# All weights of the first modulation asked for first, one of its eight row pieces summed on TensorE, and the first casts of h on ScalarE

## The chip, the cores and the metric

The kernel runs on one core of one Trainium2 chip. The core has five engines that run side by side, each through its own list of instructions in a fixed order: TensorE (PE in the profile, its weight loads PEld), VectorE (DVE), ScalarE (ACT), GpSimd (POOL) and SyncE (SP), which here only asks for transfers (DMAs). The metric is the device time of one execution in microseconds (us); less is better.

## The reference

One layer of a decoder trunk over 2048 positions of width 1024. The part that the change touches is the beginning: the modulation of the input c, the normed and modulated input h, and the first projection.

```python
c_act = jax.nn.silu(c)
mod = c_act @ w_ada[l] + b_ada[l]
sh1, sc1, gt1, sh2, sc2, gt2 = [m[:, None, :] for m in jnp.split(mod, 6, axis=-1)]
h = rms_norm(x, g_mix[l]) * (1.0 + sc1) + sh1
y = hybrid_mixer(h, w_in[l], ...)      # p = h @ w_in, then attention, mLSTM, spatial gating, w_out
x = x + gt1 * y
h = rms_norm(x, g_ffn[l]) * (1.0 + sc2) + sh2
x = x + gt2 * conv_ffn(h, w_up[l], w_conv[l], b_conv[l], w_down[l])
```

The matrix w_ada is 1024 x 6144. Only the columns of sh1 and sc1 (the first 2048) are needed before h exists.

## The kernel before

**Precision.** A product of two float32 matrices is made of three: each operand is split into a high part in a reduced format (a cast: hh, wh) and the rest (a subtraction: hl, wl), and `mm3` (lines 53 to 56) issues high x high, high x low and low x high into one PSUM bank.

**The first modulation.** `first_mod(hf)` makes half of sh1 and sc1: hf = 0 gives the columns for row pieces 0 to 3 of h, hf = 1 those for pieces 4 to 7. For each of its two column groups n (512 columns of w_ada) `load_ada` asks for eight tiles wa of 128 rows x 512 columns, 256 KB each, one for each row piece k of c. `mod_sum` on DVE adds them up, each row weighted by cs, the column of silu(c) (one instruction a tile, lines 418 and 420), into modacc; four products with a column of ones (line 441) then add over the 128 rows and leave the result as columns in PSUM. Three small DVE instructions (lines 445 to 447) make sh1 and a1, the scale. The 24 short rows of b_ada and g_mix are turned on PE (line 393) and copied (line 396) for this.

**h.** `make_h(tb)` works on a block of 512 positions. `norm_x` norms four x tiles of 128 positions: two squares with sums on ACT (jk, line 518), small DVE steps, a power on POOL (line 128), and the scaling on DVE (line 523). For each of eight row pieces k PE turns four 128 x 128 tiles (line 560), ACT applies a1 and sh1 (h, line 564), DVE casts (hh, line 565) and subtracts (hl, line 566). Block 0 takes pieces k = 0 to 3 from the first half of the modulation and k = 4 to 7 from the second.

**The first projection.** The weights of the first column block (256 columns of km and 16 gate columns: 272) come as wr, two requests for each of eight row pieces (line 585); ACT casts them (wh, line 595), POOL subtracts (wl, line 596). Then 24 products of 272 columns per 128 positions make one tile acc, which ACT copies out (ev, line 661), while DVE takes the gates. Eight such tiles use blocks 0 and 1; the next column block has products of 512 columns.

**Beside it** stand small set-up steps: casts of the identity, of selector rows and of two masks (identb, selb, maskb, maskT; maskf takes the buffer that the 24 rows had), and `head_setup`, which turns the spatial weights wsn on PE (line 549) and copies them on ACT (wT, line 550).

**What sets the order.** Up to the second column block a planner orders the instructions of each engine from the code and its own costs; from there on, the order is as written. All DMAs go through SP's list, so a request that must wait holds those behind it. Tiles come from pools with a fixed number of buffers: wa, hh and hl share 32 (hT); modacc, h and later weights share four (t2k).

## Time and profile before

| what | value |
|---|---|
| median of 3 runs | 2607.26 us (2603.63 to 2610.91) |
| profiled execution | 2607.8 us, of which the span from first to last instruction is 2606.1 us |
| TensorE busy | 2530.5 us, 97% of the span |
| VectorE busy | 2010.0 us, 77% |
| ScalarE busy | 1272.8 us, 49% |
| GpSimd busy | 402.5 us, 15% |
| chain that ended last | PE 81%, DVE 9%, DMA 4%, ACT 3% |

The page gives shares over the whole span; the change lies in the first 80 us, so the views to read are the stages of the opening, the instructions in order of time there (columns: start, time, engine, line, operation, out<-in, shape, count, and in brackets the idle time of the engine before it with what ended it), and the groups of equal instructions (busy time, mean, idle before). Where a row holds several instructions (x8), its time is that from the first start to the last end. A row's time includes what of it overlaps the next; the pace of products is read from the distance of their starts.

### The profile page before, as it was taken

To read this page: it belongs to the slowest core of one execution; us is meant where nothing else is said; L and a number is where in the kernel's file an instruction comes from. 1 tells how busy PE (TensorE), PEld (TensorE's weight loads), DVE (VectorE), ACT (ScalarE), POOL (GpSimd) and SP (SyncE) were. 2 spreads that over 40 slices of the span, in tenths; PEclk is the share of its full clock that TensorE was granted. 3 is DMA by queue.
4 is the path that set the end of the run, shared out by engine and by line. 5 is a ranking of instruction groups with operands and counts; after the bars stand their busy time and mean duration, and the time that the engine had idled before them with its cause. 6 is when DMAs were issued, how large, how long until landed. Compare 5 with 4: busy or idle time off the path is not lost.

```text
span 2606.1 us, 36311 instructions
## 1 busy us (share of the span) xinstructions
PE 2530.5 (97%) x12521; PEld 2097.9 (81%) x12537; DVE 2010.0 (77%) x3438; ACT 1272.8 (49%) x2424; POOL 402.5 (15%) x532
## 2 busy tenths in 40 slices
PE   5999999999999999999989999999999999999999
PEld 5888888888787877777868888888888888888787
DVE  7657666476388889866589888888888887997797
ACT  4333343432388878844455544454444444444443
POOL 2012310132266556520000000000000000000000
PEclk9999999999999999999999999999999999999999
DMA  7345763454664445266632222255222217658523
GB/s 247 107 120 160 209 209 88 129 152 138 180 164 123 129 126 166 58 195 224 248 89 92 79 89 82 81 201 187 90 81 81 90 65 279 210 176 290 184 93 117
DMA packets 302592, 379.58 MB, mean 146 GB/s; under 512 B 31934, under 2 KB 194588, under 8 KB 300360
## 3 DMA queue, kind: packets, MB, share of 16 engines
q1 hardware_dynamic: 302408, 377.26, 46.1%
q8 instruction: 99, 1.62, 0.3%
q14 instruction: 85, 0.70, 0.1%
HBM read 276.44 MB, written 100.74 MB: 145 GB/s over the span
## 4 chain that ended last, share of the span: by engine, by line
PE 81%; DVE 9%; DMA 4%; ACT 3%; issue 2%; POOL 1%; SPq 0%; DVEq 0%; ACTq 0%; POOLq 0%
PE ub L56 11%; PE ub L54 11%; PE ub L55 11%; PE acc L54 6%; PE acc L56 6%; PE acc L55 6%; PE db L55 4%; PE db L56 4%; PE db L54 4%; PE sp L206 3%; PE tp L259 3%; PE op L245 2%; PE op L246 2%; PE wps L55 2%; PE wps L54 2%
## 5 line engine op out<-in xcount | busy, mean ns | idle before, releaser
L54 PE MATMUL acc<-wh,hh 128*128 128x512 f32 (+2 forms) x768 | 285.5, 373 | 1.9 <-DVE vhl L762 1.2
L54 PE MATMUL ub<-T,wsph 128*128 128x512 f32 x704 | 274.2, 390 | 5.8 <-ACT wsph L1358 5.8
L56 PE MATMUL ub<-T,wspl 128*128 128x512 f32 x704 | 273.7, 389 | 1.6 <-DVE wspl L1359 1.6
L56 PE MATMUL acc<-wh,hl 128*128 128x512 f32 (+2 forms) x768 | 274.2, 360 | 0.3 <-DVE hl L566 0.3
L55 PE MATMUL acc<-wl,hh 128*128 128x512 f32 (+2 forms) x768 | 273.9, 358 | 0.2
L55 PE MATMUL ub<-T,wsph 128*128 128x512 f32 x704 | 273.9, 389 | 0.0
L55 PE MATMUL db<-wspl,wsph 128*128 128x512 f32 x616 | 240.6, 391 | 3.6 <-DVE wspl L1490 3.5
L56 PE MATMUL db<-wsph,wspl 128*128 128x512 f32 x616 | 239.6, 389 | 0.0
L54 PE MATMUL db<-wsph 128*128 128x512 f32 x616 | 238.3, 389 | 0.3 <-ACT wsph L1489 0.3
L1358 ACT CAST wsph<-S 128x512 fp32r<-128x512 f32 x176 | 109.7, 623 | 228.4 <-PE ub L55 162.8
L263 DVE TENSOR_TENSOR plo<-tp,phi 128x512 fp32r<-128x512 f32 (+1 forms) x320 | 187.0, 607 | 31.6 <-ACT phi L262 29.4
L54 PE MATMUL ub<-B,wsph 128*128 128x512 f32 x528 | 207.1, 392 | 2.8 <-ACT wsph L1358 2.8
L56 PE MATMUL ub<-B,wspl 128*128 128x512 f32 x528 | 207.2, 392 | 0.6 <-DVE wspl L1359 0.6
L55 PE MATMUL ub<-B,wsph 128*128 128x512 f32 x528 | 207.0, 392 | 0.0
L223 ACT ACTIVATE L<-L,nm 128x1024 f32<-128x1024 f32 (+2 forms) x192 | 172.6, 903 | 36.0 <-DVE nm L212 34.7
L262 ACT CAST phi<-tp 128x512 fp32r<-128x512 f32 (+1 forms) x320 | 160.0, 521 | 40.2 <-PE tp L259 38.9
L259 PE MATMUL tp<-ident,L 128*128 128x128 f32 x1088 | 177.0, 274 | 2.5 <-POOL L L228 0.6
L206 PE MATMUL sp<-kk,q 128*128 128x512 f32 (+3 forms) x640 | 169.2, 375 | 3.3 <-DVE nm L212 2.2
L1489 ACT CAST wsph<-act 128x512 fp32r<-128x512 f32 x132 | 82.3, 623 | 179.0 <-PE db L55 162.2
L228 POOL TENSOR_SCALAR L<-L,rs 128x1024 f32<-128x1024 f32 (+2 forms) x192 | 167.2, 881 | 11.0
L56 PEld LDWEIGHTS acc<-wh,hl 128*128 128x128 f32 x768 | 145.0, 190 | 22.3 <-DVE hl L566 0.8
L54 PEld LDWEIGHTS acc<-wh,hh 128*128 128x128 f32 x768 | 146.2, 191 | 20.7 <-DVE vhl L762 1.4
(333 smaller groups left out, 5942.9 us busy)
## 6 DMA issues: line engine op xcount, KB each, us to landing
w<-in_w_up_dram SPq DMA_DIRECT2D x88, 512.0 KB
wd<-in_w_down_dram SPq DMA_DIRECT2D x176, 256.0 KB
wa<-in_w_ada_dram SPq DMA_DIRECT2D x96, 256.0 KB
act_d<-yc SPq DMA_DIRECT2D x44, 512.0 KB
act<-act_d SPq DMA_DIRECT2D x44, 512.0 KB
wr<-in_w_in_dram SPq DMA_DIRECT2D x64, 256.0 KB
q<-q_d SPq DMA_DIRECT2D x128, 128.0 KB
hc_d<-hl SPq DMA_DIRECT2D x28, 512.0 KB
```

The lines of the kernel that those rows point to most:

```text
L54: T.matmul(ps, lh, rh, start=start, stop=False, skip_group_check=resume)
L55: T.matmul(ps, lh, rl, start=False, stop=False, skip_group_check=resume)
L56: T.matmul(ps, ll, rh, start=False, stop=stop, skip_group_check=resume)
L206: T.matmul(sp[:, b : b + bw], q2[n][:, qs], kk[:, s0 + b : s0 + b + bw], start=n == 0, stop=n == 1 and not last)
L223: A.activation(L[c], L[c], AF.Exp, bias=nm[:, n - 1 : n], scale=-1.0, accum_out=rs[:, c : c + 1])
L228: G.tensor_scalar(t, t, rs[:, 0:1], 1.0, op0=ALU.mult, op1=ALU.mult)
L245: T.matmul(op[:, c0:], vv[:, j, :], hi[:, c0:], start=(j == 0), stop=False)
L259: T.transpose(tp[:, i * P : (i + 1) * P], rows[i][j // 8][:, (j % 8) * P : (j % 8 + 1) * P], ident)
L262: A.copy(hi[:, c0:], tp[:, c0:])
L263: V.tensor_tensor(lo[:, c0:], tp[:, c0:], hi[:, c0:].bitcast(F32), op=ALU.subtract)
L1358: A.copy(hi, src)
L1489: A.copy(hi, v)
```

## The change

- Both halves of the modulation ask for their 32 wa tiles before the first column weights. The 16 gate columns come in one request (gw) and are copied into the eight weight tiles by POOL; SP's list has 16 wa, 2 rows, 16 wa, gw, 8 wr where it had 16 wa, 2 rows, 16 wr, 16 wa.
- Of the eight row pieces of each column group DVE sums seven; the eighth goes to PE: four products of the wa tile itself with the column of cs. All products add onto a bank that DVE has set to zero.
- The eight hh casts of block 0 move from DVE to ACT.
- The casts of identb, selb, maskb and maskT move from DVE to POOL.

The order on DVE at the end of the second half of the modulation, before. Each modacc_409 row is one step of the sum of its second column group, with the wa tile that it takes; h32_446, h32_457 and h32_468 are row pieces 0 to 2 of h in block 0 with their hh and hl; sh1 and a1 are shift and scale:

```order
L420 SCALAR_TENSOR_TENSOR modacc_409<-wa_419,cs_92,modacc_409 128x512
L565 CAST hh_447<-h32_446 128x512
L420 SCALAR_TENSOR_TENSOR modacc_409<-wa_422,cs_92,modacc_409 128x512
L566 TENSOR_TENSOR hl_448<-h32_446,hh_447 128x512
L420 SCALAR_TENSOR_TENSOR modacc_409<-wa_425,cs_92,modacc_409 128x512
L565 CAST hh_458<-h32_457 128x512
L420 SCALAR_TENSOR_TENSOR modacc_409<-wa_428,cs_92,modacc_409 128x512
L566 TENSOR_TENSOR hl_459<-h32_457,hh_458 128x512
L420 SCALAR_TENSOR_TENSOR modacc_409<-wa_431,cs_92,modacc_409 128x512
L565 CAST hh_469<-h32_468 128x512
L445 TENSOR_TENSOR sh1_89<-mps_166,colA_86 128x4
L446 TENSOR_TENSOR a1_88<-mps_166,colA_86 128x4
```

And with the change, where the sum is modacc_437 and pieces 0 to 3 are h32_461, h32_472, h32_483 and h32_494:

```order
L446 SCALAR_TENSOR_TENSOR modacc_437<-wa_309,cs_92,modacc_437 128x512
L579 TENSOR_TENSOR hl_463<-h32_461,hh_462 128x512
L446 SCALAR_TENSOR_TENSOR modacc_437<-wa_311,cs_92,modacc_437 128x512
L579 TENSOR_TENSOR hl_474<-h32_472,hh_473 128x512
L446 SCALAR_TENSOR_TENSOR modacc_437<-wa_313,cs_92,modacc_437 128x512
L579 TENSOR_TENSOR hl_485<-h32_483,hh_484 128x512
L453 TENSOR_TENSOR sh1_89<-mps_166,colA_86 128x4
L454 TENSOR_TENSOR a1_88<-mps_166,colA_86 128x4
L579 TENSOR_TENSOR hl_496<-h32_494,hh_495 128x512
L455 SCALAR_TENSOR_TENSOR a1_88<-a1_88,colA_86 128x4
```

The casts are gone from DVE's list, only the subtractions (hl) still stand among the steps, and each group's sum is one step shorter.

The order on ACT from the second half's h (pieces 4 to 7) to the statistics jk of the next four x tiles, before:

```order
L564 ACTIVATE h_490<-trp,sh_89,a_88 128x512
L564 ACTIVATE h_501<-acc,sh_89,a_88 128x512
L564 ACTIVATE h_512<-trp,sh_89,a_88 128x512
L564 ACTIVATE h_523<-acc,sh_89,a_88 128x512
L550 COPY wT<-mp 128x512
L518 ACTIVATE jk,st<-xt 128x512 x2
L661 COPY ev<-acc 128x256
```

With the change; the row ahead of the first is h_505, piece 4:

```order
L608 CAST wh<-wr 128x272 x4
L576 CAST hh<-h_505 128x512
L608 CAST wh<-wr 128x272
L574 ACTIVATE h_516<-acc,sh_89,a_88 128x512
L574 ACTIVATE h_527<-trp,sh_89,a_88 128x512
L576 CAST hh<-h_516 128x512
L574 ACTIVATE h_538<-acc,sh_89,a_88 128x512
L576 CAST hh<-h_527 128x512
L576 CAST hh<-h_538 128x512
L674 COPY ev<-acc 128x256 x2
L560 COPY wT<-mp 128x512
L526 ACTIVATE jk,st<-xt 128x512 x2
```

Five weight casts and the four hh casts now stand between and behind the h of the upper half (before, all eight weight casts stood ahead of the first h), and the copies of two finished tiles come ahead of wT and jk.

The order on PE around the turn of wsn, which wT copies, before (acc_689 and acc_721 are the first two tiles of 128 positions):

```order
L54 MATMUL acc_721<-wh_356,hh_469 128x272
L55 MATMUL acc_721<-wl_357,hh_469 128x272
L56 MATMUL acc_721<-wh_356,hl_470 128x272
L54 MATMUL acc_721<-wh_360,hh_480 128x272
L549 MATMUL mp_551<-ident_74,wsn_545 128x128 x4
L56 MATMUL acc_689<-wh_368,hl_503 128x272
```

With the change (acc_768 is the third tile of 128 positions):

```order
L56 MATMUL acc_768<-wh_393,hl_474 128x272
L54 MATMUL acc_768<-wh_397,hh_484 128x272
L55 MATMUL acc_768<-wl_398,hh_484 128x272
L559 MATMUL mp_566<-ident_74,wsn_560 128x128 x4
L56 MATMUL acc_768<-wh_397,hl_485 128x272
```

The turn of wsn stood behind 27 products of 272 columns and now stands behind 56. From the first product of 512 columns on, the orders of all engines are the same as before.

The diff:

```diff
-    V.tensor_copy(identb, ident)
+    G.tensor_copy(identb, ident)
...
-    def mod_sum(tiles):
-
-        acc = pool.tile([P, 512], F32, name="modacc", tag="t2k")
-        for k, st in enumerate(tiles):
-            if k == 0:
-                V.tensor_scalar(acc, st, cs[:, 0:1], None, op0=ALU.mult)
-            else:
-                V.scalar_tensor_tensor(acc, st, cs[:, k : k + 1], acc, op0=ALU.mult, op1=ALU.add)
-        return acc
...
-    def first_mod(hf):
+    V.memset(modp[:, 0:16], 0.0)
+
+    def first_load(hf):
+        return {n: list(load_ada(n * 512, "hT")) for n in (hf, 2 + hf)}
+
+    def first_mod(hf, tiles):
         for n in (hf, 2 + hf):
-            acc = mod_sum(load_ada(n * 512, "hT"))
-            for j in range(4):
-                T.matmul(modp[:, n * 4 + j : n * 4 + j + 1], acc[:, j * P : (j + 1) * P], ones[:, 0:1], start=True, stop=True)
+            acc = pool.tile([P, 512], F32, name="modacc", tag="t2k")
+
+            def add(w, col):
+                for j in range(4):
+                    T.matmul(
+                        modp[:, n * 4 + j : n * 4 + j + 1], w[:, j * P : (j + 1) * P], col,
+                        start=False, stop=True, skip_group_check=True,
+                    )
+
+            for k, st in enumerate(tiles[n]):
+                if k == 0:
+                    V.tensor_scalar(acc, st, cs[:, 0:1], None, op0=ALU.mult)
+                elif k < 7:
+                    V.scalar_tensor_tensor(acc, st, cs[:, k : k + 1], acc, op0=ALU.mult, op1=ALU.add)
+                else:
+                    add(st, cs[:, k : k + 1])
+            add(acc, ones[:, 0:1])
...
-    first_mod(0)
+    ada = first_load(0)
+    first_mod(0, ada)
+    ada = first_load(1)
...
-            V.tensor_copy(hh, h32)
+            if tb == 0:
+                A.copy(hh, h32)
+            else:
+                V.tensor_copy(hh, h32)
...
-        def load(self):
+        def load(self, n=2):
...
-            for col, wd in self.parts:
+            for col, wd in self.parts[:n]:
...
-        V.tensor_copy(selb[r : r + 4], bc(ident[r : r + 4, r : r + 4], 2, P))
+        G.tensor_copy(selb[r : r + 4], bc(ident[r : r + 4, r : r + 4], 2, P))
...
-    V.tensor_copy(maskb, m32)
+    G.tensor_copy(maskb, m32)
...
-    V.tensor_copy(maskT, bc(maskf, 1, 4))
+    G.tensor_copy(maskT, bc(maskf, 1, 4))
...
+    gw = pool.tile([P, KT, 16], F32, name="gw", tag="tmpA")
+    dma(gw, w_in[:, C_G : C_G + 16].rearrange("(k p) n -> p k n", p=P))
     for k in range(KT):
-        cur.load()
+        cur.load(1)
+        G.tensor_copy(cur.raw[k][:, 256:272], gw[:, k, :])
     for k in range(KT):
         cur.cast()
-    first_mod(1)
+    first_mod(1, ada)
```

## The prediction

> **What bounds the kernel now.** I read the page first, then the opening by stages, then its instructions in order of time.

> ```profile
> span 2606.1 us, 36311 instructions
> PE   5999999999999999999989999999999999999999
> ```

> TensorE (PE) is full in every slice of 65 us but the first, so the kernel ends as early as PE's fixed stream of products is fed. The change touches only the opening; whatever it saves or loses by the moment PE is full for good is carried to the end. The stages (columns: stretch, its length, busy time and count for PE, weight loads, VectorE (DVE), ScalarE (ACT), GpSimd (POOL), granted clock, DMA share, GB/s):

> ```profile
> 10.00:20.00 10.00, 4.13 (x16) 2.78 (x15) 8.83 (x20) 1.86 (x7) 2.42 (x4) 1.00 1.03 371
> 20.00:30.00 10.00, 3.96 (x17) 3.75 (x17) 7.81 (x14) 3.34 (x8) 6.67 (x9) 1.00 0.74 197
> 30.00:40.00 10.00, 3.32 (x16) 3.32 (x17) 9.64 (x15) 2.23 (x3) 0.83 (x2) 1.00 0.85 308
> 47.00:53.00 6.00, 6.00 (x26) 5.67 (x27) 5.08 (x12) 2.79 (x5) 0.35 (x1) 1.00 0.66 258
> 60.00:72.00 12.00, 12.00 (x96) 11.66 (x95) 11.18 (x25) 7.96 (x14) 0.55 (x1) 1.00 0.53 154
> ```

> PE is fed from 47 us on. Before that DVE is the busy engine, with the row sums of the first modulation, and it is nearly full again from 60 to 72, with the second block of h. So there are two gates, and a gain at the first is kept only if the second does not close. Does DVE wait for data in the first?

> ```profile
> L420 DVE SCALAR_TENSOR_TENSOR modacc<-wa,cs,modacc 128x512 f32<-128x512 f32 x28 | 21.6, 780 | 0.5
> 16.47 8.64 SPq L585 DMA_DIRECT2D wr<-in_w_in_dram x16
> 25.16 9.75 SPq L410 DMA_DIRECT2D wa<-in_w_ada_dram  x16
> ```

> Hardly: 0.5 us of idle before 28 sums of 780 ns. So asking for the second sixteen wa tiles at 16.5 instead of 25.2 us gains nothing by itself; I cost it at 0, covered by the sums ahead of it. The price is that wr, whose 16 requests become 9, is asked for after wa; its casts are then queued behind h, which comes back below.

> **First gate: DVE's sums, then ACT.**

> ```profile
> 24.05 0.97 DVE L839 CAST maskT<-maskf 128x512 bf16<-128x512 f32 x1 [0.18 <-POOL maskf L838]
> 24.95 2.41 DVE L420 SCALAR_TENSOR_TENSOR modacc<-wa,cs,modacc 128x512 f32<-128x512 f32 x2
> 23.99 6.84 POOL L596 TENSOR_TENSOR wl<-wr,wh 128x272 fp32r<-128x272 f32 x8
> 29.58 0.56 DVE L447 SCALAR_TENSOR_TENSOR a<-a,colA 128x4 f32<-128x4 f32 x1
> 30.06 1.06 DVE L418 TENSOR_SCALAR modacc<-wa,cs 128x512 f32<-128x512 f32 x1
> 36.54 0.48 DVE L418 TENSOR_SCALAR modacc<-wa,cs 128x512 f32<-128x512 f32 x1
> L565 DVE CAST hh<-h 128x512 fp32r<-128x512 f32 x7 | 2.9, 419 | 0.0
> ```

> First half of the modulation: two sums leave DVE (2 x 0.78 = 1.56), the mask casts go to POOL (0.97 + 0.18 of waiting, and a 0.22 one), and the two last sums, 2.41 us beside POOL's wl, go back to 1.56 since wl now comes later: 3.8 us. Against that, POOL's identity and selector casts stand ahead of the rsqrt of the x tiles, and one x scaling stands behind a later statistic: 0.7 us, an estimate from the length of one scaling (0.76, below). PE's turn of the 24 column rows now comes after the last sum instead of ahead of it: 0.3 and 0.2 for its copy. The scale a is 0.3 quicker alone (0.56 against 0.25 for the second one). Net: a is ready 2.9 us earlier, at 27.2.

> Second half: two sums (1.56) and the first two hh casts (0.84) leave DVE's queue, and the first term is 1.06 only beside POOL, 0.48 alone (0.58): 3.0 us. New beside it are POOL's late mask work and eight small gw copies, since the wait of maskf's buffer for the 24 rows now lasts until 26.6. How much these hold DVE isn't shown; the nearest rows lost 0.4 to 0.6 us per instruction beside wl. I take 0.6 in all, bounds 0 and 3. Net 2.4, in sum 5.3.

> [...]

> TensorE's added products (k = 7, four per piece) are as long as those of the sum, of which four take 1.87 us (x8 records below); three of the four groups run while PE waits for DVE, the last ahead of its sum too, so 0.

> ```profile
> 27.41 1.87 PE L441 MATMUL mps<-ones,modacc 128*128 128x1 f32 x8 [4.43 <-DVE modacc L420]
> 43.16 0.75 DVE L420 SCALAR_TENSOR_TENSOR modacc<-wa,cs,modacc 128x512 f32<-128x512 f32 x1
> 46.98 0.78 ACT L564 ACTIVATE h<-trp,sh,a 128x512 f32<-128x512 f32 x1 [5.13 <-DVE a L447]
> 48.30 0.69 DVE L566 TENSOR_TENSOR hl<-h,hh 128x512 fp32r<-128x512 f32 x1
> 48.94 0.43 PE L54 MATMUL acc<-wh,hh 128*128 128x272 f32 x1
> 49.17 0.43 PE L55 MATMUL acc<-wl,hh 128*128 128x272 f32 x1
> 63.40 0.62 ACT L595 CAST wh<-wr 128x512 fp32r<-128x512 f32 x1
> 25.87 0.42 ACT L595 CAST wh<-wr 128x272 fp32r<-128x272 f32 x1 [0.28 <-DMA wr<-in_w_in_dram]
> ```

> So the last sum ends at 43.9 - 5.3 = 38.6, and h of the fifth piece starts at 46.98 - 5.3 = 41.7. Before, its hl ended at 48.99, 2.0 later. Now ACT runs, after that h (0.68 apart), four wh casts (4 x 0.42) and hh at the price of a 128x512 cast (0.6), then DVE the hl (0.69): 3.6, so 45.3. ACT's new work thus gives back 1.6 of the 5.3. Queued behind the h that waits for a are these wh casts, and behind those POOL's wl of pieces 3 to 7 (0.75 to 0.86 each), which follow at about PE's pace; bounds for that 0 and 1. With the last product of the piece PE has 15 products done at 45.6; before, the sixteenth starts at 49.17. First gate: 3.5 us earlier (bounds 0.1 and 4.1).

> **Second gate: ACT's queue.** The statistics of the next four x tiles (jk, the squares) stand on ACT behind the copy wT, and wT waits for PE's turn of wsn.

> ```profile
> 51.89 1.05 PE L549 MATMUL mp<-ident,wsn 128*128 128x128 f32 x4
> 52.98 0.59 ACT L550 COPY wT<-mp 128x512 f32<-128x512 f32 x1 [3.21 <-PE mp L549]
> 53.46 0.64 ACT L518 ACTIVATE jk<-xt 128x512 f32<-128x512 f32 x1
> 60.88 0.76 DVE L523 TENSOR_SCALAR xt<-xt,st 128x1024 f32<-128x1024 f32 x1 [0.58 <-POOL st L128]
> 71.73 0.69 DVE L566 TENSOR_TENSOR hl<-h,hh 128x512 fp32r<-128x512 f32 x1
> 72.64 0.54 PE L56 MATMUL acc<-wh,hl 128*128 128x272 f32 x3
> 78.28 0.39 PE L54 MATMUL acc<-hh,wh 128*128 128x512 f32 x1
> 51.44 0.43 PE L56 MATMUL acc<-wh,hl 128*128 128x272 f32 x1
> 51.66 0.43 PE L54 MATMUL acc<-wh,hh 128*128 128x272 f32 x1
> 58.75 0.29 PE L54 MATMUL acc<-wh,hh 128*128 128x272 f32 x1
> 58.88 0.29 PE L55 MATMUL acc<-wl,hh 128*128 128x272 f32 x1
> ```

> From the first jk (53.46) runs one serial chain: scale xt, turn, h, hh, hl on a full DVE; its last hl ends at 72.42, PE uses it at 72.64, and the first product of the next block starts at 78.28, 24.8 us after jk. PE keeps busy with the first block's products meanwhile, and has no slack to the last hl.

> In the changed order 56 products stand ahead of the wsn turn instead of 27 (the PE rows shown above). With 15 done at 45.6, 41 remain. Starts lie 0.22 to 0.23 us apart up to about 53 us and 0.13 after, with a granted clock of 1.00 in both stretches. Before, the slow stretch lasted some 5.6 us after PE began to run without gaps (47.5). I take the same: until 51.2 PE does 23 or 24 products and the small turn of 16 rows, then 17.5 x 0.125 = 2.2, and 0.5 for wsn: 53.9, against 52.94. So jk starts 1.0 us later although PE started 3.5 us earlier. With no slow stretch, 41 x 0.125 gives 51.4 (1.5 earlier); slow throughout, 41 x 0.226 and a slow turn give 56.0 (3.1 later). I keep the middle. The chain behind jk has the same instructions, so the next block starts at 79.3: **+1.0 us**. PE alone would be there at 78.28 - 3.5 + 0.9 (1.7 us more at half pace) = 75.7; the 3.6 us between turn up as waits of PE for xt and hl, about 59 to 73 us. From that block on the orders are the same.

> Sum against the profiled execution: span 2606.1 + 1.0 = 2607.1. That execution took 2607.8, 0.5 over the median of the runs, 2607.26; the median becomes 2608.3. With the first gate's bounds (3.4 worse, 0.6 better) and the slow stretch's (2.1 worse, 2.5 better) the shift lies between -2.1 and +6.5; the runs before spread by 3.6 either way.

> **Rivals.**
> - *The first gate's gain is kept.* If PE runs at full pace early, or ACT gets through its casts faster, jk starts no later than before and the gain is what PE alone allows: 2.6 us, 2604.7. For it: PE is full from 47 us and DVE's relief is real. Against: only a jk 1 to 3 us earlier than before gives it, which needs nearly the fast bound.
> - *PE falls back to its slow pace at the second gate.* The waits are on PE, near 60 us; if the pace drops there, the 42 products behind the last hl cost 0.1 more each, 4.2 us, beside the 1.0: 2612.5, slower. It decides if PE's waits for xt join into one long gap. For it: 7.4 us without work at 29 to 37 us had slow products on both sides. Against: I expect the waits singly, some 1.6 us each, the pitch of the xt scalings.
> - *DVE is held by POOL for long.* At the bound of 3 us the first gate gains 1.1, jk comes 3.4 later: 2610.7.
> - *The early requests do nothing and the late wr starves POOL:* included, as the 0 and the bound of 1 above.

> [...]

> **Chances.** The small loss 0.55, the kept gain 0.2, the slow pace 0.1, POOL's hold 0.1, something unseen 0.05. All four prices are under 0.3% (7.8 us), about what a measurement of this kernel can tell from no change: so within it 0.77. The losses can add up (1.0 + 4.2 + 2.4 = 7.6) and run spread does the rest: slower by more 0.14. Faster by more needs three times what PE allows: 0.09, for what I may not see. The range takes the cases from 2604.7 to 2612.5 and most of the spread: 2602 to 2615.

> **What would show it.** Second a near 41.6, first h of the upper half near 41.7, sixteenth product near 45.6; ACT's wT and jk near 54 to 55; PE idle for some 3 us in pieces between 59 and 73; first 512-wide product of the next block near 79. Wrong if that product comes before 76 or after 83, if PE's idle sits elsewhere, or if stages after 100 us differ.

## The result, and the profile after

The changed kernel takes 2612.79 us in the median of 8 runs (2609.62 to 2615.10); the kernel before took 2605.93 us in the median of 8 runs beside it (2603.63 to 2610.91). The ratio is 1.0024, with a 95% interval from 1.0015 to 1.0034. That lies within the 0.3% that the prediction took as the bound of no change, but outside zero: a small loss. A second job put it at 1.0013 (1.0005 to 1.0022). Over all runs the changed kernel averages 2612.0 us (19 runs) and the kernel before 2607.9 (118 runs): 4.1 us apart, plus or minus 1.0.

Two lines of the page of the changed kernel:

```profile
span 2611.3 us, 36387 instructions
PE   6999999999999999999989999999999999999999
```

Its span is 5.2 us above the 2606.1 before. The instructions of the changed opening in order of time, with DVE, ACT and PE mixed (columns as before; of the lines named in the prediction, L455 is now the second step of a, L574 h, L559 the turn of wsn, L526 the squares):

```profile
38.31 0.74 DVE L446 SCALAR_TENSOR_TENSOR modacc<-wa,cs,modacc 128x512 f32<-128x512 f32 x1
41.16 1.24 DVE L579 TENSOR_TENSOR hl<-h,hh 128x512 fp32r<-128x512 f32 x1
42.32 0.15 DVE L455 SCALAR_TENSOR_TENSOR a<-a,colA 128x4 f32<-128x4 f32 x1
42.57 0.78 ACT L574 ACTIVATE h<-trp,sh,a 128x512 f32<-128x512 f32 x1 [2.64 <-DVE a L455]
46.30 0.47 PE L54 MATMUL acc<-wh,hh 128*128 128x272 f32 x1
53.45 0.60 PE L559 MATMUL mp<-ident,wsn 128*128 128x128 f32 x4
54.57 0.64 ACT L526 ACTIVATE jk<-xt 128x512 f32<-128x512 f32 x1
61.24 0.44 PE L570 MATMUL trp<-ident,xt 128*128 128x128 f32 x2 [0.97 <-DVE xt L531]
62.91 0.44 PE L570 MATMUL trp<-ident,xt 128*128 128x128 f32 x2 [1.23 <-DVE xt L531]
64.11 1.11 PE L570 MATMUL trp<-ident,xt 128*128 128x128 f32 x4 [0.76 <-ACT h L574]
72.95 0.69 DVE L579 TENSOR_TENSOR hl<-h,hh 128x512 fp32r<-128x512 f32 x1
80.19 0.39 PE L54 MATMUL acc<-hh,wh 128*128 128x512 f32 x1
```

The first gate opens earlier: the second half's a is ready at 42.3 instead of 46.6, and the sixteenth product starts at 46.30, before at 49.17. The second gate opens later: jk at 54.57, before 53.46. PE waits for x tiles, and the next block's first product starts 1.9 us later than before (78.28). The other 3.3 us of the span came after that, and not in one place. By the starts of the same ScalarE instructions, the changed kernel is 1.9 us behind at 200 us, 3.5 at 300, 4.1 at 1000, 7.3 at 1300, 5.6 from 1400 to 2200 and 4.9 at the end. These are stretches of 3.41 us around the waits of the opening and around the first wait behind it that costs time, in the changed kernel (columns: stretch, length, busy time of PE, PEld, DVE, ACT, POOL, granted clock, DMA share, GB/s):

```profile
60.16:63.58 3.42, 0.98 (x5) 0.40 (x4) 2.45 (x7) 1.59 (x4) 0.78 (x2) 1.00 0.12 38
63.58:66.99 3.41, 2.88 (x13) 2.88 (x14) 3.38 (x7) 2.85 (x5) 0.00 (x0) 0.50 0.56 154
66.99:70.40 3.41, 3.41 (x30) 3.41 (x30) 3.34 (x8) 2.87 (x5) 0.00 (x0) 1.00 0.48 123
213.76:217.18 3.42, 0.73 (x8) 0.75 (x8) 3.24 (x7) 1.49 (x4) 1.55 (x2) 1.00 0.88 308
217.18:220.59 3.41, 3.41 (x12) 2.73 (x11) 2.80 (x8) 0.00 (x0) 1.44 (x2) 0.50 0.16 56
```

and at the second place in the kernel before:

```profile
210.10:213.51 3.41, 1.74 (x8) 1.10 (x6) 2.87 (x7) 1.85 (x5) 2.67 (x3) 1.00 0.71 222
213.51:216.93 3.42, 2.40 (x15) 2.16 (x16) 3.34 (x7) 0.43 (x1) 1.05 (x2) 1.00 0.53 196
```

In these rows the granted clock is 1.00 or 0.50 in whole stretches of 3.41 us. In the changed kernel PE had nothing to do for 2.69 of the 3.42 us from 213.76, and the next 3.41 us ran at half clock. The kernel before has the same wait (the instruction that ended it, first before, then after):

```profile
214.53 1.06 PE L1052 MATMUL mps<-ident,hq 128*128 128x128 f32 x8 [2.69 <-DVE hq L1045]
```

```profile
216.47 1.28 PE L1065 MATMUL mps<-ident,hq 128*128 128x128 f32 x8 [2.69 <-DVE hq L1058]
```

There it lay across two stretches, 1.67 us in one and 1.02 in the next, and the clock stayed at 1.00. The next transposes of the same kind show what that cost: 296.03 before, 299.52 after, so 3.5 us apart, where the ones above are 1.9 apart.

```profile
296.03 1.09 PE L1052 MATMUL mps<-ident,hq 128*128 128x128 f32 x8 [0.88 <-DVE hq L1045]
```

```profile
299.52 1.09 PE L1065 MATMUL mps<-ident,hq 128*128 128x128 f32 x8 [0.88 <-DVE hq L1058]
```

Up to 1300 us the changed kernel's profile has half-clock stretches at 63.6, 217.2, 1029.5 and 1237.8 us; that of the kernel before has one, at 1230.7. Between 1300 and 1350 us each has three more.

### The profile page after: what moved, and what is told of

The parts are those of the page before. It is cut to its first block, busy times and chain, and to the rows that moved or that the text cites. A ratio compares the mean times of both kernels' runs of the same rounds, so it can differ in the third digit from the quotient of the medians.

```text
span 2611.3 us, 36387 instructions
## 1 busy us (share of the span) xinstructions
PE 2539.3 (97%) x12569; PEld 2107.6 (81%) x12569; DVE 2001.9 (77%) x3421; ACT 1276.7 (49%) x2432; POOL 408.5 (16%) x546
## 4 chain that ended last, share of the span: by engine, by line
PE 81%; DVE 8%; DMA 4%; issue 3%; ACT 2%; POOL 1%; SPq 0%; DVEq 0%; ACTq 0%; POOLq 0%
PE ub L56 11%; PE ub L54 10%; PE ub L55 10%; PE acc L54 6%; PE acc L55 6%; PE acc L56 6%; PE db L55 4%; PE sp L206 4%; PE db L56 4%; PE db L54 4%; PE tp L259 3%; PE op L245 2%; PE op L246 2%; PE wps L55 2%; PE wps L54 2%
## 5 line engine op out<-in xcount | busy, mean ns | idle before, releaser
L54 PE MATMUL acc<-wh,hh 128*128 128x512 f32 (+2 forms) x768 | 286.3, 375 | 1.7 <-DVE vhl L775 1.2
L54 PE MATMUL ub<-T,wsph 128*128 128x512 f32 x704 | 274.3, 390 | 5.8 <-ACT wsph L1374 5.8
L56 PE MATMUL acc<-wh,hl 128*128 128x512 f32 (+2 forms) x768 | 274.6, 361 | 0.5 <-DVE st L529 0.5
L56 PE MATMUL ub<-T,wspl 128*128 128x512 f32 x704 | 273.7, 389 | 0.9 <-DVE wspl L1375 0.9
L55 PE MATMUL acc<-wl,hh 128*128 128x512 f32 (+2 forms) x768 | 273.8, 359 | 0.4 <-POOL wl L609 0.2
L55 PE MATMUL ub<-T,wsph 128*128 128x512 f32 x704 | 273.9, 389 | 0.0
L55 PE MATMUL db<-wspl,wsph 128*128 128x512 f32 x616 | 240.4, 390 | 3.5 <-DVE wspl L1506 3.5
L56 PE MATMUL db<-wsph,wspl 128*128 128x512 f32 x616 | 239.7, 389 | 0.0
L54 PE MATMUL db<-wsph 128*128 128x512 f32 x616 | 238.2, 389 | 0.3 <-ACT wsph L1505 0.3
L54 PE MATMUL ub<-B,wsph 128*128 128x512 f32 x528 | 207.0, 392 | 2.8 <-ACT wsph L1374 2.8
L56 PE MATMUL ub<-B,wspl 128*128 128x512 f32 x528 | 206.8, 392 | 0.4 <-DVE wspl L1375 0.4
L55 PE MATMUL ub<-B,wsph 128*128 128x512 f32 x528 | 206.6, 391 | 0.0
L56 PEld LDWEIGHTS acc<-wh,hl 128*128 128x128 f32 x768 | 145.8, 191 | 22.4 <-DVE hl L579 1.0
L54 PEld LDWEIGHTS acc<-wh,hh 128*128 128x128 f32 x768 | 146.9, 192 | 20.4 <-DVE vhl L775 1.4
```

What stands on the lines that cost most here:

```text
L54: T.matmul(ps, lh, rh, start=start, stop=False, skip_group_check=resume)
L55: T.matmul(ps, lh, rl, start=False, stop=False, skip_group_check=resume)
L56: T.matmul(ps, ll, rh, start=False, stop=stop, skip_group_check=resume)
```

## Experiments

The first moves the set-up in the changed kernel, and the next three take one part back out of it; then two run both kernels once more; the last six fill waits, move them against the clock's stretches, or join two of these edits. Times of a job stand beside the kernel before on the same chip, 33 runs in each of three jobs (medians 2608.06, 2607.86 and 2608.41 us). "The 512-wide product" is the one at 78.28 us before and 80.19 after.

**e1: the set-up behind the second block's h.** jk no longer stands behind wT.

```diff
             make_h(half * 2, x0)
+            make_h(half * 2 + 1)
             if half == 0:
                 head_setup()
-            make_h(half * 2 + 1)
```

> The changed kernel with the head set-up (turn of wsn, copy wT) written behind the second block of h, so that on ScalarE the jk statistics stand right behind the first block's casts. Theory (the second gate: jk waits for wT, wT for PE's 56 products): jk starts near 49 instead of 54.6 us, PE's waits at 60 to 66 us and the half-pace window at 63.6 us go, the first 512-wide product comes at 75.5 to 77 us instead of 80.2, and the time is 3 to 5 us under the changed kernel, 1.5 to 3 us under the kernel before on that account alone. Rival (the lost time lies elsewhere, in half-pace windows after 100 us or in the first modulation): the 512-wide product stays within 1 us of 80.2, the time within 1.5 us of the changed kernel's.

2610.55 us, ratio 1.0002 (0.9993 to 1.0010). jk and the 512-wide product:

```profile
47.85 0.65 ACT L526 ACTIVATE jk<-xt 128x512 f32<-128x512 f32 x1
76.98 0.39 PE L54 MATMUL acc<-hh,wh 128*128 128x512 f32 x1
```

The opening ends 3.2 us earlier than in the changed kernel and 1.3 earlier than before (0.7 against the mean of the four profiles of that opening further down). So the second gate is real, and with it gone the first gate's gain comes through in part. But the time is not below the kernel before, where 1.5 to 3 us under it were expected. This profile has half-clock stretches at 214.3, 1026.7 and 1187.1 us; how much of the gain they took is not shown.

**e2: the requests in the order of before** (16 wr with their gate columns ahead of the second 16 wa; no gw and no copies on POOL).

```diff
     first_mod(0, ada)
-    ada = first_load(1)
...
-        cur.load(1)
-        G.tensor_copy(cur.raw[k][:, 256:272], gw[:, k, :])
+        cur.load()
...
-    first_mod(1, ada)
+    first_mod(1, first_load(1))
```

> The changed kernel with the column weights asked for ahead of the second modulation half again, with two requests a tile; the product of the eighth piece on PE, the casts on ScalarE and the masks on GpSimd stay. The wsn turn then stands behind 34 products instead of 56. Second-gate theory: jk near 52 us, 512-wide product near 77, 1 to 2 us under the kernel before. Rival (the early requests are what helps DVE): the second scale a comes 2 us or more later than 42.5 us and the 512-wide product at 80 or later.

2612.19 us, ratio 1.0015 (1.0005 to 1.0024). The second half's a, jk and the 512-wide product:

```profile
44.91 0.16 DVE L455 SCALAR_TENSOR_TENSOR a<-a,colA 128x4 f32<-128x4 f32 x1
52.87 0.64 ACT L526 ACTIVATE jk<-xt 128x512 f32<-128x512 f32 x1
77.80 0.40 PE L54 MATMUL acc<-hh,wh 128*128 128x512 f32 x1
```

The first gate opens 2.6 us later than in the changed kernel. DVE now waits for wa tiles ahead of four of its sums, 1.4 us in all, so the early requests were worth something there. The opening ends 2.4 us earlier all the same, since only 34 products stand ahead of the turn of wsn, where the changed kernel has 56. The earlier first gate is bought with a later second one. The profiled execution keeps most of this: its span is 2609.3 us, 2.0 under that of the changed kernel, and both have six half-clock stretches behind the opening (here at 375.9, 546.6 and 1027.9 us, and three past 1300). But the 11 runs average 2612.5 us, where the changed kernel has 2612.0, and 1 to 2 us under the kernel before were expected. An opening that ends level with that of the kernel before thus did not bring its time; what took the gain in the other runs is not shown.

**e3: the hh casts of block 0 back on DVE.**

```diff
-            if tb == 0:
-                A.copy(hh, h32)
-            else:
-                V.tensor_copy(hh, h32)
+            V.tensor_copy(hh, h32)
```

> The changed kernel with the first block's hh casts on VectorE again; all else stays. The wsn turn now stands behind 65 products. Second-gate theory: jk 1 to 2 us later than 54.6, 512-wide product at 81 to 82.5 us, 1 to 2 us over the changed kernel. Rival (the casts on ScalarE hold up the upper half of h and cost the time): the 512-wide product comes earlier than 79 us.

2613.42 us, ratio 1.0023 (1.0013 to 1.0033). a at 40.01, 2.3 us earlier than in the changed kernel, but 65 products ahead of wsn's turn, jk at 55.91, and

```profile
82.87 0.39 PE L54 MATMUL acc<-hh,wh 128*128 128x512 f32 x1
```

2.7 us later. The later jk makes 1.3 of them; with the rest goes the clock, which was at half for two stretches here (from 64.51 us) and for one in the changed kernel. The earlier a did not bring the end of the opening forward.

**e4: the casts of identb, selb, maskb and maskT back on DVE.**

```diff
-    G.tensor_copy(maskT, bc(maskf, 1, 4))
+    V.tensor_copy(maskT, bc(maskf, 1, 4))
...
```

> The changed kernel with the identity, selector and mask casts on VectorE again; the wsn turn stays behind 56 products. Theory: VectorE waited for the 24 rows anyway, so the first a moves by at most 1.5 us and the 512-wide product stays at 79.5 to 81.5. [...]

2612.11 us, ratio 1.0014 (1.0005 to 1.0023). a at 41.70, jk at 53.36, and the 512-wide product at 80.30, where the changed kernel has 80.19. In this profile the move gains nothing at the opening's end, but two differences cancel: the clock went full at 47.97 us instead of 49.92, with jk 1.2 us earlier, and behind jk it was at half for two stretches (from 61.63 us) instead of one. What the casts alone are worth there is not shown; the time is that of the changed kernel.

**n1 and n2: both kernels once more, unchanged.**

> The kernel before, unchanged, for a second profile. Grid theory: the granted clock moves in stretches of 3.41 us whose grid lies differently in each execution, and a TensorE wait of 2 to 3 us halves it only if the wait falls right on the grid; so the half-clock stretches between 200 and 1300 us, of which the first profile had one (1230.7), lie elsewhere now or differ in number (0 to 4), and the 512-wide product that began at 78.28 begins within 77.5 to 80. Rival, a fixed loss of the changed kernel past the opening: the stretches lie where they lay (1230.7 alone up to 1300), and nothing moves by over 0.3 us.

> The changed kernel, unchanged, for a second profile. Grid theory: half-clock stretches between 200 and 1300 us at other places than 217.2, 1029.5 and 1237.8, 1 to 4 of them; the 512-wide product that began at 80.19 between 79.5 and 82, as the second gate holds in every execution and only the clock around it moves. Rival, a fixed loss: stretches at the same three places, and the distance to the kernel before 6 to 7 us at 1300 us again.

2606.65 us (ratio 0.9995, 0.9986 to 1.0004) and 2610.73 us (1.0013, 1.0005 to 1.0022). The expectation that the half-clock stretches lie elsewhere in each execution fell. Up to 1300 us the kernel before has one again, at 1229.8; the changed kernel has 65.6, 219.2, 1031.6 and 1239.8 again, each 2.0 us later than in its first profile, and a new one at 550.3. So most of them come with the kernel. The rival did not hold as it stood either: the 512-wide product started at 81.39 instead of 80.19. The stretches at the wait for hq in the second profile, first before:

```profile
209.22:212.63 3.41, 2.13 (x10) 1.40 (x8) 2.87 (x6) 1.67 (x4) 2.67 (x3) 1.00 0.67 213
212.63:216.05 3.42, 2.02 (x13) 1.88 (x14) 3.35 (x8) 0.62 (x1) 1.05 (x2) 1.00 0.65 235
```

then after:

```profile
215.78:219.19 3.41, 1.22 (x10) 1.20 (x11) 3.34 (x8) 0.90 (x3) 1.44 (x1) 1.00 0.86 318
219.19:222.60 3.41, 3.41 (x10) 2.63 (x9) 2.80 (x7) 0.00 (x0) 1.94 (x2) 0.50 0.06 18
```

Before: 1.28 and 1.40 us idle, clock 1.00. After: 2.19 us idle in one stretch, and the next at 0.50.

**n3 and n4: four long waits filled, in the changed kernel and in the one before.** The transposes write where the next ones write over them.

```diff
             yp = mps()
+            if j == 0 and qi in (0, 2):
+                for n in range(18):
+                    T.transpose(yp[:, n % 4 * P : (n % 4 + 1) * P], ident, ident)
...
+            fill, into = {1: (22, "X"), 2: (38, "Z")}.get(p, (0, "X")) if first else (0, "X")
+            for k in range(fill):
+                T.transpose(getattr(self, into)[:, k % 4 * P : (k % 4 + 1) * P], ident, ident)
```

> The changed kernel with idle transposes of the identity into the four longest TensorE waits past the opening: 18 in front of the transposes of hq for row blocks 0 and 2 (waits of 2.69 us at 214 and 546 us in before) and 22 and 38 in front of the first and third product of the up projection (2.81 us at 1316, 4.60 at 1332). Their results are overwritten. Grid theory: no half-clock stretch at 214 to 220, 546 to 553, 1319 to 1347; the time falls by 4 to 7 us against the changed kernel, to 2606 to 2609, and so below or level with before. If the stretches cost nothing beside the waits themselves: time unchanged, 2612 to 2613.

> The kernel before with the same idle transposes in the same four waits. Grid theory: the difference to n3 shrinks to what the opening costs, 1 to 3 us, as the places at which the grid can charge either kernel are mostly gone; time 2603 to 2606. If the changed kernel had a fixed loss past the opening beside it, n3 stays 5 us or more above this run.

2607.36 us (ratio 0.9998, 0.9989 to 1.0007) and 2606.41 us (0.9996, 0.9987 to 1.0004). The means are 2607.4 and 2606.1: 4.6 us under the changed kernel's mean, 1.8 under that of the kernel before, and 1.3 apart, with some 2 us of uncertainty. The filled wait in n3:

```profile
214.70 2.12 PE L1066 MATMUL mps<-ident 128*128 128x128 f32 x18
217.45 1.09 PE L1068 MATMUL mps<-ident,hq 128*128 128x128 f32 x8 [0.63 <-DVE hq L1058]
```

and the stretch behind it:

```profile
218.97:222.38 3.41, 3.41 (x17) 2.80 (x16) 2.83 (x7) 0.60 (x1) 2.15 (x2) 1.00 0.03 11
```

PE still had to wait until 217.45 for hq. All that changed is that it was busy meanwhile, and no half-clock stretch followed here, at 546 us or at the two waits near 1320. It was not the waits themselves that cost here, but the half clock behind them: the time fell by 4.6 us, though these transposes started as far behind the 512-wide product as in the changed kernel (136.2 and 136.3 us).

**s1 and s2: the same wait moved against the stretches.** 14 idle transposes ahead of the third column block in the kernel before, 19 in the changed one.

```diff
     for n, (half, i) in enumerate(steps):
+        if n == 2:
+            ps = mps()
+            for k in range(14):
+                T.transpose(ps[:, k % 4 * P : (k % 4 + 1) * P], ident, ident)
```

> The kernel before with 14 idle transposes of the identity (1.6 us at 0.115 us each) in front of the third column block, about 140 us in: everything behind them moves by 1.6 us against the grid of 3.41 us. Window theory: the stretches hang on how much of one grid window TensorE is idle, with about 2.0 us as the point from which the next window is halved; in the two profiles of before the 2.69 us wait for hq at 214 us lay over two windows (1.67 and 1.02 us, 1.28 and 1.40) and cost nothing; moved by 1.6 it lies in one. So a half-clock stretch begins at 215 to 219 us, and the shift against before is 1.6 us at 200 us and 3.1 at 240. Rival, waits alone decide and not where they lie: no stretch there, shift 1.6 at both places. Total 2609 to 2612 by the first (later waits fall anew), 2608 to 2610 by the second.

> The changed kernel with 19 such transposes (2.2 us) at the same place. Window theory: in its two profiles the wait at 214 us lay 2.69 and 2.20 us in one window and halved the next; moved by 2.2 it lies over two, with less than 1.8 us in either, so no half-clock stretch at 215 to 223 us, and of the 2.2 us that the transposes cost only 0.7 are left at 240 us. At 546 us a stretch may come instead. Total within 1.5 us of the changed kernel. Rival, waits alone: stretch still there, shift 2.2 at 240 us.

2610.44 us (ratio 1.0007, 0.9998 to 1.0016) and 2613.02 us (1.0020, 1.0011 to 1.0029). The stretches of s1, the kernel before with the wait moved into one of them:

```profile
211.55:214.96 3.41, 0.71 (x6) 0.42 (x5) 2.92 (x6) 1.73 (x5) 1.86 (x2) 1.00 0.92 341
214.96:218.38 3.42, 3.42 (x13) 2.94 (x11) 2.81 (x9) 0.00 (x0) 1.12 (x2) 0.50 0.09 35
```

and of s2, the changed kernel with the wait moved across two:

```profile
213.80:217.21 3.41, 1.61 (x7) 0.97 (x6) 2.87 (x7) 1.92 (x5) 2.67 (x3) 1.00 0.73 215
217.21:220.62 3.41, 2.50 (x15) 2.25 (x16) 3.23 (x7) 0.36 (x1) 1.04 (x2) 1.00 0.53 190
```

Both came as the window theory said: in s1 2.70 us of idle in one stretch and 0.50 in the next, in s2 1.80 and 0.91 us in two stretches and 1.00 in both. The second transposes of hq, which stood at 296.03 and 299.52, show the price:

```profile
297.65 1.09 PE L1052 MATMUL mps<-ident,hq 128*128 128x128 f32 x8 [0.89 <-DVE hq L1045]
```

```profile
299.61 1.09 PE L1065 MATMUL mps<-ident,hq 128*128 128x128 f32 x8 [0.89 <-DVE hq L1058]
```

In s1 the first transposes started at 214.57, level with before (214.53): this execution's opening ended 1.2 us earlier (77.11) and the transposes took that. From there to the second ones a further 1.6 us were lost. In s2 the first ones started at 218.12, 1.65 behind the changed kernel, the second 0.09 behind: 1.6 us won by adding 2.2 us of work. One halved stretch cost about 1.6 us here.

**c1 and c2: both edits together.** The set-up as in e1 and the four waits filled, in the changed kernel and in the one before.

> The changed kernel with head_setup behind the second block's h (as in e1) and the four long waits filled (as in n3). If the two costs add: e1 took 3.3 us off the changed kernel and n3 5.4 off its time by medians, so 2603 to 2606, below before. If the windows of the opening and the later ones were one cost counted twice: 2606 to 2608.

> The kernel before with head_setup behind the second block's h and the four waits filled. If the second gate also holds the kernel before, its 512-wide product, at 77.4 to 78.3 us in three profiles, begins by 77 and the time is 2604 to 2606, level with c1 or above it by the first gate's gain of about 1 us; if the gate binds only where the products behind it are late, as in the changed kernel, the time is that of n4, 2605 to 2607.

2608.44 us (ratio 0.9999, 0.9990 to 1.0007) and 2609.57 us (1.0004, 0.9995 to 1.0012). Neither beats the kernel before, and each lies above both times that were forecast for it. In c1 the opening ends at 77.14, but new half-clock stretches stand at 374.7, 681.9 (two in a row) and 1357.7 us. In c2 the first jk comes at 41.99, ahead of the second half's a, and yet the 512-wide product starts at 79.16, later than in any profile of before. Between 44 and 80 us PE waits only 1.1 us in all, so there the second gate does not bind. Its sixteenth product starts at 50.39, 1.2 us later than before; why is not shown.

## Why the prediction was right, and where it was not

The sign and the range hold: a small loss, through the opening in part. But the loss is of about 4 us and not of 1; the range, drawn wide enough for the rivals, caught a size that the sum did not have. Step by step:

- **First gate: right in kind, 0.7 us short.** a was forecast at 41.6 and came at 42.3; the sixteenth product was forecast near 45.6 and came at 46.30. Already the first half's a was ready at 27.86 instead of 27.2: its sums ended at 25.03, where the prediction's terms give 24.3, so the terms up to there were 0.7 us too good. The last sum ended at 39.05 instead of 38.6, and an hl of 1.24 us stood between the two steps of a (the rows at 41.16 and 42.32). The upper bound of 3 us for POOL's hold on DVE is a term that no run shows: in the second half four sums beside seven of POOL's gw copies took 3.11 us, 0.78 each as before, and only that hl, beside POOL's wl, was 0.56 longer than the 0.68 of the three ahead of it. The buffer wait of maskf did not hold POOL until 26.6: its last mask cast, at 18.32, took 1.04 us and POOL then idled until gw. Costing the early requests at nothing was wrong: with them undone a came 2.6 us later (e2). DVE's 0.5 us of idle showed only that the old order of requests kept up with the old, longer queue of DVE; in e2 the shorter queue waited 1.4 us for wa.
- **Second gate: right in kind, the place of jk in part by luck.** jk was forecast at 54.5 and came at 54.57. Two misses cancelled: PE's sixteenth product started 0.7 us late, and the slow stretch, forecast to last until 51.2, ended at 49.92. What the slow pace is, the prediction misread. It gave a granted clock of 1.00 for both paces, but in these two profiles the clock is on record only from 53.08 us (before) and 49.92 us (after), and the views print 1.00 where nothing is on record. Within 0.7 us of these moments the starts of PE's products go from 0.23 to 0.12 or 0.13 us apart. The record of s1 begins earlier and shows the clock in the slow stretch:

```profile
47.70:51.11 3.41, 3.41 (x16) 3.41 (x16) 3.34 (x8) 1.30 (x2) 0.04 (x1) 0.50 0.86 334
51.11:54.52 3.41, 3.41 (x30) 3.41 (x29) 0.89 (x4) 2.71 (x9) 0.43 (x1) 1.00 0.01 3
```

 So the slow pace is the half clock, and its end differs from one execution to the next (table). e1, e2 and e3 moved jk both ways, and the 512-wide product followed; a did not decide it. In the kernel before, PE waits only 0.3 us between 47 and 80 us: the second gate hardly binds there, and in the changed kernel it costs PE 3.3 us of waits.
- **Its size was 1.0 us, and measured 3.1.** Four profiles of each opening (of the kernels before and after, and of the four whose edits lie behind it) give, in us:

| opening of | clock full from | jk | 512-wide product | from jk to it |
|---|---|---|---|---|
| before, n1, n4, s1 | 53.08, 52.20, 50.88, 51.11 | 53.46, 52.98, 52.57, 52.29 | 78.28, 77.79, 77.37, 77.11 | 24.8 in each |
| after, n2, n3, s2 | 49.92, 51.94, 51.73, 49.96 | 54.57, 55.47, 55.37, 54.52 | 80.19, 81.39, 81.29, 80.16 | 25.6 to 25.9 |
| mean difference | -0.9 | 2.2 | 3.1 | 1.0 |

 jk was 1.1 later against the profile that was forecast from, and 2.2 over four: that profile's opening was the latest of its four. The chain behind jk was forecast to have the same length, and grew by 1.0.
- **That 1.0 is the second rival, in part.** PE did fall back to half pace at the second gate, from 63.58 to 66.99, for one stretch. The rival priced it at 4.2 and let it decide only if the waits join into one long gap. They came singly, 0.97, 1.23 and 0.76 us, as forecast; 2.44 us of idle in one stretch of 3.42, with 0.98 us of work in it, was enough.
- **The step that failed: "From that block on the orders are the same".** The orders are, but the time is not, and one of the prediction's own signs of being wrong, stages that differ after 100 us, came true. The opening now ends at another point of the clock's 3.41 us stretches, so waits that were free before are followed by half clock now. s1 and s2 show it for the wait at 214 us, by turning it on in one kernel and off in the other. From the opening to the end the first two profiles drew a further 3.3 us apart, the second two 4.6 (spans 2603.2 and 2611.4, less the opening's 3.6). Not all of that need be the clock: the second profile of the kernel before is 1.1 us ahead of its first at 1329 us and 2.9 at the end, with the same mean clock in both from 1200 to 1400 us (0.97) and from 1400 to 2400 (1.00). Over the runs, 4.1 us in all less 3.1 for the opening leave about 1 us, if the opening's delay is kept to the end. n3 and n4 give another figure: filling the four waits took 4.6 us off one kernel and 1.8 off the other, so these waits cost the changed kernel some 2.8 us more, uncertain by 2.2. And e2 has the opening of the kernel before with the time of the changed one. So both parts are real, by e1 and by s1 and s2, but how the 4.1 us divide between them stays open.

## What to carry to other kernels

When one serial stage feeds another engine's queue, count what the new order puts ahead of the second stage: e2 had the slower first gate and the faster opening. A gain of a few us in the opening of a kernel that is bound by TensorE can be lost where the later waits fall worse on the clock's stretches (about 1.6 us here at the wait at 214 us), so read the granted clock stretch by stretch, in two profiles of each kernel, before a difference of one to five us is explained. Take a printed clock of 1.00 for full clock only where the pace of the products agrees (starts 0.23 us apart here at half clock, 0.12 or 0.13 at full). Where TensorE must wait for 2 us or more, work whose result nobody reads can be cheaper than idling: four waits filled with it took 4.6 us off the changed kernel (n3).
